# Two lanes of experts in a float32 network: subtractions a piece later, spread products in the lane's own banks, a spaced gather, another order of chunks

## The chip, the cores and the metric

One Trainium2 chip, and of it one core. The metric is the device time of one execution of the whole program in microseconds (us); lower is better. Every matrix product runs on TensorE (PE), elementwise work on VectorE (DVE) and ScalarE (ACT), a little on GpSimd (POOL); SyncE (SP) issues the loads of the weights.

## The reference, cut to what matters

The network is two blocks on 256 tokens of width 1024, in float32. The change touches only its last part, a mixture of eight experts, two of them for each token:

```python
def swiglu(t, w_gate, w_up, w_down):
    return jnp.matmul(jax.nn.silu(jnp.matmul(t, w_gate)) * jnp.matmul(t, w_up), w_down)

def moe_swiglu(h, w_router, w_gate, w_up, w_down):      # t [256, 1024], 8 experts, 3584 hidden
    logits = jnp.matmul(t, w_router)
    top_val, top_idx = lax.top_k(logits, 2)
    gates = jax.nn.softmax(top_val, axis=-1)
    combine = jnp.sum(jax.nn.one_hot(top_idx, 8) * gates[..., None], axis=1)
    for e in range(8):
        out = out + combine[:, e:e + 1] * swiglu(t, w_gate[e], w_up[e], w_down[e])
```

## The kernel before

**Pieces.** The weights of an expert are read in tiles of 128 x 2048 floats, 1 MB, here called pieces. An expert has seven chunks of 512 hidden columns; a chunk is two pieces of the gate weights (`w_eg`), two of the up weights (`w_eu`) and two of the down weights (`w_ed`). All eight experts are 336 pieces. SP loads a piece into one of nine buffers (`raw`). To multiply in float32 precision, a piece is split in two: ACT copies it to `wh`, rounded (L341), and DVE subtracts, `wl = raw - wh` (L342). Both go to "wide" buffers, four of each. PE then multiplies with `wh` and with `wl`. The subtraction is the last reader of `raw`, so it lets SP load the next piece; PE's products are the last readers of the wide buffers, so they let ACT copy the piece four further on.

**Two lanes.** The experts are sorted by the number of their tokens. The first three (`BIG`) are the lane 0, with up to 128 tokens each: PE needs 12 products of 512 columns for a piece (L289 to L291: high by high, low by high, high by low). The other five are lane 1, with up to 64 tokens: high and low part of the tokens stand side by side in the 128 columns of the stationary operand, and a piece takes 8 products (L1164, L1165); their two halves are added by one more product with a constant (`fold`, L1256). `two_lanes` sets the order of the chunks: four chunks of lane 0, then two of lane 1 and one of lane 0 in turn, at the end one of lane 1.

**What follows a chunk.** After a chunk's projections: `silu` on ACT, `times` on DVE (`h`, L1263), four transposes on PE (L1268, into a `tp` bank), and `parts`, which splits the transposed tile into `hT` (ACT, then DVE). The down products of a chunk stand behind the projections of the chunk that follows it, and sum up in two banks (`acc`) for each lane. After an expert's last chunk, for each half of the columns, `scaled` splits the sum into `y` (ACT L344, DVE L345), `spread` multiplies it back to the token rows (PE L1225) and adds it to `x` (DVE L381). The next expert's (or two small experts') tokens are gathered by `collect`: `pick` (a one-hot `G` on DVE), four `turn`s (8 or 16 short products, L1130), four copies to `xg` (ACT), `back` (transposes of `G`, then `gs` and `GT` on DVE).

**Order.** It is written by hand: a list of pieces, and for each piece a list of steps (`at(i, f)`) that come behind it. The driver runs over i; it first issues load, copy and subtraction of piece i + 3, then the products of piece i, then the steps listed for i. `in_order` chains the instructions of PE, ACT and DVE in just that order, so an engine never overtakes an instruction that waits.

**PSUM banks.** Four `acc` (two for each lane), two `pr` (projections), two `tp`. The transposes, the gather, `back` and `spread` share the two `tp` banks.

Of the kernel before, what the change touches and what calls it, by code (L numbers as in the profile page):

```python
# [193 lines left out]
class Net:  # L194
# [53 lines left out]
    def piece(self, ap, w=2048, scales=None, pool=None, fine=False):  # L248
# [5 lines left out]
        with ExitStack() as st:  # L254
# [754 lines left out]
    def moe(self, R):  # L1009
# [12 lines left out]
        with ExitStack() as st:  # L1022
# [16 lines left out]
            v.tensor_scalar(g1, g2, 1.0, None, op0=OP.add)  # L1039
            v.reciprocal(g1, g1)  # L1040
            v.tensor_tensor(g2, g2, g1, op=OP.mult)
            v.tensor_tensor(comb, sel, oh0, op=OP.subtract)
            v.tensor_tensor(comb, comb, b2(g2), op=OP.mult)
            v.tensor_tensor(oh0, oh0, b2(g1), op=OP.mult)
            v.tensor_tensor(comb, comb, oh0, op=OP.add)
# [6 lines left out]
            for ins, n in zip((R.scored[1, 1], R.counted), self.dummies):  # L1052
                self.keep_warm(R.xh[:, 0, :P], R.xh[:, 0, :512], (ins,), n)
            first = self.gather_first(self.slot(0), G, comb)
# [3 lines left out]
            v.tensor_scalar(c1[:, 1:], count[:, 1:], 1.0, None, op0=OP.mult)  # L1058
            v.tensor_scalar(c1[:, :1], count[:, :1], float(2 * T), None, op0=OP.add)
            place = self.places(c1)  # L1060
# [4 lines left out]
            v.tensor_tensor(which, index[:, :, None].to_broadcast([P, NE, NE]), place[:, None, :].to_broadcast([P, NE, NE]),  # L1065
                            op=OP.is_equal)
            v.tensor_tensor(prod[:, 0], which, index[:, None, :].to_broadcast([P, NE, NE]), op=OP.mult)
            v.tensor_reduce(ids, prod[:, 0], axis=AX.X, op=OP.add)
            v.tensor_copy(idi, ids)
            kcp = mo.tile([P, 4, NE], F32, name="kcp")  # L1070
            v.tensor_tensor(prod, kc.rearrange("p a t e -> p (a t) e")[:, :, None, :].to_broadcast([P, 4, NE, NE]),
                            which[:, None].to_broadcast([P, 4, NE, NE]), op=OP.mult)
            v.tensor_reduce(kcp, prod, axis=AX.X, op=OP.add)
            self.less = mo.tile([P, NE], F32, name="less")
            v.tensor_scalar(self.less, place, BIG - 0.5, float(P - HALF), op0=OP.is_gt, op1=OP.mult)
            v.tensor_tensor(c1, count, self.less, op=OP.add)
            most = mo.tile([P, 1], F32, name="most")
            v.tensor_reduce(most, c1, axis=AX.X, op=OP.max)
            mosti = mo.tile([P, 1], I32, name="mosti")
            v.tensor_copy(mosti, most)  # L1080
            self.experts(first, idi, kcp[:, :2], kcp[:, 2:])
# [22 lines left out]
    def back(self, G, comb, k, dt):  # L1104
# [8 lines left out]
        GT = mo.tile([P, T], dt, name="GT", bufs=5)  # L1113
# [28 lines left out]
    def gather_first(self, slot, G, comb):  # L1142
# [4 lines left out]
        return [((slot[:, :KB], slot[:, KB:]),) + self.back(G[:, :, 0], comb, 0, F32R)]  # L1147
# [31 lines left out]
    def experts(self, first, idi, key, comb):  # L1179
# [4 lines left out]
        ids, found = {0: 0}, {0: first[0]}  # L1184
# [11 lines left out]
        def collect(small, k, i):  # L1196
# [4 lines left out]
            def pick():  # L1201
                s["G"], s["x"] = self.pick(key, k, n, small), self.slot(small)
# [7 lines left out]
            def back(e):  # L1210
                x = s["x"].rearrange("p (e k) m -> p k e m", e=2)[:, :, e] if small else (s["x"][:, :KB], s["x"][:, KB:])
                found[k + e] = (x,) + self.back(s["G"][:, :, e], comb, k + e, F32R)

            at(i, pick)
            for j in range(4):
                at(i + 1 + j, lambda j=j: turn(j))
# [343 lines left out]
```

## Time and profile before

| what | value |
|---|---|
| median of 3 runs | 1823.81 us (1821.02 to 1824.0) |
| the profiled execution: its own time | 1823.72 us |
| its span, from first to last instruction | 1821.6 us |
| mean granted TensorE clock | 0.979 of 2.4 GHz |
| busy: PE, DVE, ACT | 1733.0, 1502.6, 1247.2 us |
| part of the experts: first product to last split in the pattern | about 903 to 1784 us of the span |

Times in the rows below count from the start of the span. "Busy" of PE is modelled: its matmuls are pipelined, and a row's duration is longer than the distance to the next one. DMA share is the mean busy share of the 16 DMA engines; a wait in square brackets is the engine's idle time before an instruction and what ended it.

### The profile page before, as it was taken

The page shows a single profiled execution, that of the slowest core. Times are in us where ns is not written, and L with a number is a line of the kernel's source. Part 1 is how long each engine was busy: PE and PEld are TensorE (multiplying, and loading weights), DVE is VectorE, ACT ScalarE, POOL GpSimd, SP SyncE. Part 2 cuts the span into 40 slices and gives each one's busy share as a digit, 9 for nine tenths or more (in the row PEclk, how much of TensorE's full clock was granted, in tenths as well). Part 3 has the DMA queues.
Part 4 walks back from the last instruction along what each step waited for, and adds up shares of the span by engine and source line. Part 5 has one row for each costly group of instructions (what it writes and reads, how often), then busy time and mean ns, then how long its engine had stood idle before and what let it go on. Part 6 is the DMA issues. An engine that isn't in the chain of part 4 may idle for free.

```text
span 1821.6 us, 23787 instructions
## 1 busy us (share of the span) xinstructions
PE 1733.0 (95%) x8735; PEld 1435.8 (79%) x8735; DVE 1502.6 (82%) x1659; ACT 1247.2 (68%) x1412; POOL 159.0 (9%) x120
## 2 busy tenths in 40 slices
PE   8999999999999999999999999899999989999996
PEld 6888778888888889998787777677777767777774
DVE  7577668777766579996689998899999988999997
ACT  5574456555655565655478887698888867888885
POOL 1033010002000024660100000000000000000000
PEclk9999999999999999999899999999999989999998
DMA  8433455554555554337389999899999989999992
GB/s 281 161 116 139 162 191 185 187 191 154 178 185 188 176 190 139 126 127 299 144 313 372 421 421 400 305 412 422 393 392 414 421 308 360 420 421 367 420 421 86
DMA packets 72141, 501.30 MB, mean 275 GB/s; under 512 B 8257, under 2 KB 9281, under 8 KB 13266
## 3 DMA queue, kind: packets, MB, share of 16 engines
q1 hardware_dynamic: 72018, 499.71, 71.7%
q8 instruction: 71, 1.16, 0.2%
q14 instruction: 52, 0.43, 0.1%
HBM read 498.63 MB, written 1.05 MB: 274 GB/s over the span
## 4 chain that ended last, share of the span: by engine, by line
PE 75%; DVE 14%; issue 7%; ACT 3%; POOL 1%; DMA 0%; SPq 0%; DVEq 0%; ACTq 0%
DVE wl L342 8%; PE acc L289 7%; PE acc L291 7%; PE acc L290 7%; PE pr L289 5%; PE pr L291 5%; PE pr L720 5%; PE tp L720 5%; PE pr L290 5%; PE pr L1164 4%; PE pr L1165 4%; PE acc L1164 4%; PE acc L1165 3%; PE tp L721 2%; PE pr L721 2%
## 5 line engine op out<-in xcount | busy, mean ns | idle before, releaser
L342 DVE TENSOR_TENSOR wl<-raw,wh 128x2048 fp32r<-128x2048 f32 (+2 forms) x588 | 1061.8, 1833 | 166.4 <-ACT wh L341 162.8
L341 ACT ACTIVATE wh<-raw 128x2048 fp32r<-128x2048 f32 (+2 forms) x596 | 892.6, 1521 | 231.3 <-PE acc L291 74.7
L1164 PE MATMUL pr<-wh,xg 128*128 128x512 f32 x560 | 228.4, 408 | 0.0
L1165 PE MATMUL pr<-wl,xg 128*128 128x512 f32 x560 | 224.8, 401 | 0.0
L289 PE MATMUL pr<-wh,xg 128*128 128x512 f32 x336 | 137.7, 410 | 0.0
L1164 PE MATMUL acc<-wh,hT 128*128 128x512 f32 x280 | 115.4, 412 | 23.0 <-DVE hT L342 23.0
L291 PE MATMUL pr<-wh,xg 128*128 128x512 f32 x336 | 134.6, 401 | 0.0
L290 PE MATMUL pr<-wl,xg 128*128 128x512 f32 x336 | 134.6, 401 | 0.0
L1164 PEld LDWEIGHTS pr<-wh,xg 128*128 128x128 f32 x560 | 107.4, 192 | 25.5
L720 PE MATMUL pr<-xT,wh 128*128 128x512 f32 x352 | 125.4, 399 | 1.9 <-DVE xT L342 1.9
L1165 PEld LDWEIGHTS pr<-wl,xg 128*128 128x128 f32 x560 | 107.4, 192 | 24.4
L720 PE MATMUL tp<-xT,wh 128*128 128x512 f32 x352 | 125.3, 399 | 0.0
L1165 PE MATMUL acc<-wl,hT 128*128 128x512 f32 x280 | 113.6, 406 | 0.0
L289 PE MATMUL acc<-wh,xT 128*128 128x512 f32 (+3 forms) x256 | 98.8, 387 | 1.9 <-ACT xT L341 1.1
L721 PE MATMUL tp<-xT,wl 128*128 128x256 f32 x352 | 98.9, 281 | 0.0
L721 PE MATMUL pr<-xT,wl 128*128 128x256 f32 x352 | 98.8, 281 | 0.0
L291 PE MATMUL acc<-wh,xT 128*128 128x512 f32 (+3 forms) x256 | 98.6, 387 | 0.2
L290 PE MATMUL acc<-wl,xT 128*128 128x512 f32 (+3 forms) x256 | 98.3, 385 | 0.0
L1164 PEld LDWEIGHTS acc<-wh,hT 128*128 128x128 f32 x280 | 54.9, 196 | 41.6 <-DVE hT L342 29.1
L1423 POOL TENSOR_TENSOR raw<-x,raw 128x512 f32<-128x512 f32 x2 | 2.5, 1286 | 916.5 <-DVE x L381 916.5
L720 PEld LDWEIGHTS pr<-xT,wh 128*128 128x128 f32 x352 | 66.1, 188 | 18.6 <-DVE xT L342 2.4
L720 PEld LDWEIGHTS tp<-xT,wh 128*128 128x128 f32 x352 | 66.1, 188 | 16.5
(373 smaller groups left out, 3344.4 us busy)
## 6 DMA issues: line engine op xcount, KB each, us to landing
raw<-in_w_eg SPq DMA_DIRECT2D x112, 1024.0 KB, 7.9
raw<-in_w_eu SPq DMA_DIRECT2D x112, 1024.0 KB, 8.0
raw<-in_w_ed SPq DMA_DIRECT2D x110, 1024.0 KB, 8.0
raw<-in_w_ffn_in SPq DMA_DIRECT2D x22, 1024.0 KB, 4.8
raw<-in_w_dense_in SPq DMA_DIRECT2D x22, 1024.0 KB, 4.8
raw<-in_w_xbc SPq DMA_DIRECT2D x16, 1024.0 KB, 5.0
raw<-in_w_ffn_out SPq DMA_DIRECT2D x11, 1024.0 KB, 4.9
raw<-in_w_dense_out SPq DMA_DIRECT2D x11, 1024.0 KB, 4.8
```

Of the source, the lines that this page charges most:

```text
L289: mm(ps, st[0], mv[0], start=start, stop=False)
L290: mm(ps, st[0], mv[1], start=False, stop=False)
L291: self.last_mm = mm(ps, st[1], mv[0], start=False, stop=stop)
L341: a = nc.scalar.activation(h, src, AF.Copy)
L342: b = v.tensor_tensor(l, src, h.bitcast(F32), op=OP.subtract)
L720: nc.tensor.matmul(ps, wh, xT[2][:, k], start=k == 0, stop=False)
L721: nc.tensor.matmul(ps[:, 0], wl, xT[0][:, k], start=False, stop=k == KB - 1)
L1164: self.nc.tensor.matmul(ps, st, mv[0], start=start, stop=False)
L1165: self.nc.tensor.matmul(ps, st, mv[1], start=False, stop=stop)
L1423: nc.gpsimd.tensor_tensor(xn[:, t, lo], self.x[:, t, lo], g[:, lo], op=OP.mult)
```

## The change

Six edits, all in the experts' part.

1. **apart.** In `piece`, ACT's copy is issued with piece i + 3 as before, but the subtraction is put off: it is issued one piece later, behind the next piece's copy. The first four pieces, which are split in halves (`gates`), stay as they were.
2. **two_lanes.** Two chunks of lane 0 first, then for each small expert 1,1,0,1,1,0,1,1,0,1,0 (the last 0 dropped). Before, the first big expert and the first small one ended with the 13th and the 14th chunk; now with the 16th and the 12th. The second big one ended with the 34th and a small one with the 35th; now the 35th and the 34th.
3. **spread.** In the pattern it writes to the lane's own two `acc` banks instead of `tp`; `y` has four buffers instead of two; `scaled` and `spread` come 1, 2, 3 and 6 pieces after the first down piece instead of 1, 5, 4 and 8.
4. **collect.** The four `turn`s stand two pieces apart instead of one, `back` follows at 9 (and 10) instead of 5 (and 6).
5. **parts** of a small chunk come behind piece 7 instead of 8. `GT` has 4 buffers instead of 5.
6. **sort.** The sorting of the experts and the gate values (`comb`), some 25 small DVE instructions ahead of the list before, stand together at i = -1 now; the first expert's `back` moves into the list, and the first small `collect` to piece 1 instead of 8.

```diff
+                if apart:
+                    self.nc.scalar.activation(ab[0], raw, AF.Copy)
+                    return Weight(hw, [ab[0][:, :hw], ab[0][:, hw:]], [ab[1][:, :hw], ab[1][:, hw:]]), \
+                        lambda: v.tensor_tensor(ab[1], raw, ab[0].bitcast(F32), op=OP.subtract)
...
-        rest = (NE - BIG) * EC
-        n = rest // 2
-        lane = [0] * (BIG * EC - n) + [1, 1, 0] * n + [1] * (rest - 2 * n)
+        runs = [2] * (EC // 2) + [1] * (EC % 2)
+        lane = [i for _ in range(NE - BIG) for r in runs for i in [1] * r + [0]][:-1]
+        lane = [0] * (BIG * EC - lane.count(0)) + lane
...
-                at(i + 1 + j, lambda j=j: turn(j))
-                at(i + 2 + j, lambda j=j: copy(j))
+                at(i + 1 + 2 * j, lambda j=j: turn(j))
+                at(i + 2 + 2 * j, lambda j=j: copy(j))
             for e in range(n):
-                at(i + 5 + e, lambda e=e: back(e))
+                at(i + 9 + e, lambda e=e: back(e))
...
-                ps = self.tp()
+                ps = banks[t] if banks else self.tp()
...
-            y = [mo.tile([P, 512], F32R, name="y%d" % b) for b in range(2)]
+            y = [mo.tile([P, 512], F32R, name="y%d" % (2 * n + b)) for b in range(2)]
...
-                when = (2, 3, 4, 4, 5, 5, 7, 8)
+                when = (2, 3, 4, 4, 5, 5, 7, 7)
...
-                    at(i + 1 + 4 * n, lambda n=n, y=y: y.update(y=scaled(small, k, n)[0]))
-                    at(i + 4 + 4 * n, lambda n=n, y=y: spread(k, n, y["y"]))
+                    at(i + 1 + n, lambda n=n, y=y: y.update(y=scaled(small, k, n)[0]))
+                    at(i + 3 + 3 * n, lambda n=n, y=y: spread(k, n, y["y"], accs[small]))
...
-        collect(1, BIG, 8)
-        ahead, ready = self.wholes - 1, {}
+        collect(1, BIG, 1)
+        at(1, lambda: found.update({0: found[0] + self.back(G[:, :, 0], self.comb, 0, F32R)}))
+        ahead, ready, rest = self.wholes - 1, {}, {}
         for i in range(-ahead, len(pieces)):
-            if i + ahead < len(pieces):
-                ready[i + ahead] = pieces[i + ahead][0]()
+            a = i + ahead
+            if a < len(pieces):
+                if self.gates:
+                    ready[a] = self.piece(pieces[a][0]())
+                else:
+                    ready[a], rest[a] = self.piece(pieces[a][0](), apart=True)
+            if a - 1 in rest:
+                rest.pop(a - 1)()
+            if i == -1:
+                sort()
```

On DVE, in the pattern, the order before is (`h` of 64 rows is a small chunk's, `hT` of 128x4x64 its split, `wl` a subtraction):

```order
L342 TENSOR_TENSOR wl<-raw,wh 128x2048 x5
L1263 TENSOR_TENSOR h<-h,pr 64x512
L342 TENSOR_TENSOR wl<-raw,wh 128x2048 x3
L342 TENSOR_TENSOR hT_9384<-tp,hT_9384 128x4x64
L342 TENSOR_TENSOR wl<-raw,wh 128x2048 x3
L1263 TENSOR_TENSOR h<-h,pr 64x512
```

and the same stretch of the pattern in the changed kernel (L267 is the subtraction put off, L346 the split of `hT`):

```order
L267 TENSOR_TENSOR wl<-raw,wh 128x2048 x5
L1274 TENSOR_TENSOR h<-h,pr 64x512
L267 TENSOR_TENSOR wl<-raw,wh 128x2048 x2
L346 TENSOR_TENSOR hT_9448<-tp,hT_9448 128x4x64
L267 TENSOR_TENSOR wl<-raw,wh 128x2048 x4
L1274 TENSOR_TENSOR h<-h,pr 64x512
```

Two subtractions stand between `h` and a small `hT` instead of three; and as every subtraction has moved behind one piece's steps, `h` now follows the subtraction of two pieces ahead of PE, not of three.

On DVE again, where the first big expert ends, the order before is (two lanes' `y` and `x` interleaved):

```order
L345 SCALAR_TENSOR_TENSOR y_10460<-acc,gs,y_10459 128x512
L342 TENSOR_TENSOR wl<-raw,wh 128x2048 x2
L345 SCALAR_TENSOR_TENSOR y_10496<-acc,gs,y_10495 128x512
L1263 TENSOR_TENSOR h<-h,pr 64x512
L342 TENSOR_TENSOR wl<-raw,wh 128x2048
L381 TENSOR_TENSOR x<-x,tp 128x512 x2
L342 TENSOR_TENSOR wl<-raw,wh 128x2048 x2
L381 TENSOR_TENSOR x<-x,tp 128x512 x2
```

and where an expert first ends in the changed kernel:

```order
L349 SCALAR_TENSOR_TENSOR y_10186<-acc,gs,y_10185 128x512
L267 TENSOR_TENSOR wl<-raw,wh 128x2048
L349 SCALAR_TENSOR_TENSOR y_10210<-acc,gs,y_10209 128x512
L346 TENSOR_TENSOR hT_10214<-tp,hT_10213 128x512
L267 TENSOR_TENSOR wl<-raw,wh 128x2048
L385 TENSOR_TENSOR x<-x,acc 128x512 x2
L267 TENSOR_TENSOR wl<-raw,wh 128x2048 x3
L385 TENSOR_TENSOR x<-x,acc 128x512 x2
```

The additions read `acc` now, and one expert's four steps stand alone.

## Rows read from the trace of the kernel before

**Rows 1.** The page's head: span and instructions.
```profile
span 1821.6 us, 23787 instructions
```

**Rows 2.** Stretches: from:to, length, busy us of each engine (instructions), PEclk, DMA share, GB/s.
```profile
903.00:1784.00 881.00, 832.20 (x3675) 659.15 (x3675) 815.58 (x523) 723.11 (x549) 0.00 (x0) 0.98 0.97 388
903.00:975.00 72.00, 72.00 (x337) 59.01 (x337) 56.74 (x58) 49.31 (x39) 0.00 (x0) 0.97 0.87 312
1115.00:1180.00 65.00, 55.80 (x232) 43.50 (x231) 55.86 (x40) 46.52 (x38) 0.00 (x0) 0.95 0.89 326
1295.00:1335.00 40.00, 36.85 (x171) 29.49 (x171) 37.62 (x29) 33.78 (x29) 0.00 (x0) 1.00 0.97 367
1455.00:1530.00 75.00, 65.80 (x258) 50.97 (x257) 62.79 (x42) 52.41 (x42) 0.00 (x0) 0.89 0.87 320
1640.00:1680.00 40.00, 37.04 (x158) 29.36 (x157) 38.51 (x25) 33.32 (x26) 0.00 (x0) 0.96 0.97 359
```

**Rows 3.** The same view: the five stretches between those, summed.
```profile
sum 589.00, PE 564.72 PEld 446.82 DVE 564.06 ACT 507.78 POOL 0.00; mean PE 112.94 PEld 89.36 DVE 112.81 ACT 101.56 POOL 0.00
```

**Rows 4.** DVE's groups, 903 to 1784: busy, mean ns | idle before, releaser.
```profile
L342 DVE TENSOR_TENSOR wl<-raw,wh 128x2048 fp32r<-128x2048 f32 x328 | 736.9, 2284 | 53.5 <-ACT wh L341 53.1
...
L381 DVE TENSOR_TENSOR x<-x,tp 128x512 f32<-128x512 f32 x24 | 15.9, 682 | 7.0 <-PE tp L1225 7.0
...
L345 DVE SCALAR_TENSOR_TENSOR y<-acc,gs,y 128x512 fp32r<-128x512 f32 x12 | 9.0, 746 | 4.3 <-ACT y L344 4.3
```

**Rows 5.** Timeline of DVE in the pattern: start, us, what, idle before.
```profile
1003.84 4.48 DVE L342 TENSOR_TENSOR wl<-raw,wh 128x2048 fp32r<-128x2048 f32 x2
...
1012.03 2.29 DVE L342 TENSOR_TENSOR wl<-raw,wh 128x2048 fp32r<-128x2048 f32 x1 [0.81 <-ACT wh L341]
1014.24 0.68 DVE L1263 TENSOR_TENSOR h<-h,pr 128x512 f32<-128x512 f32 x1
...
1022.04 11.09 DVE L342 TENSOR_TENSOR wl<-raw,wh 128x2048 fp32r<-128x2048 f32 x5
...
1047.79 4.48 DVE L342 TENSOR_TENSOR wl<-raw,wh 128x2048 fp32r<-128x2048 f32 x2
```

**Rows 6.** Timeline of PE: opening, first small piece, products in the pattern.
```profile
902.71 0.73 PE L289 MATMUL pr<-wh,xg 128*128 128x512 f32 x1
...
973.49 0.48 PE L1164 MATMUL pr<-wh,xg 128*128 128x512 f32 x1
...
1001.31 0.39 PE L291 MATMUL pr<-wh,xg 128*128 128x512 f32 x1
...
1001.54 0.40 PE L289 MATMUL pr<-wh,xg 128*128 128x512 f32 x1
...
1012.40 0.40 PE L291 MATMUL pr<-wh,xg 128*128 128x512 f32 x1
```

**Rows 7.** DMA, 1000 to 1100; landing of `raw`, 1000 to 1030, 1060 to 1090.
```profile
DMA packets 5780, 42.09 MB, mean 421 GB/s; under 512 B 646, under 2 KB 646, under 8 KB 646
...
DMA to landing us min/median/max: 7.7/8.4/9.1
...
DMA to landing us min/median/max: 8.9/9.9/10.7
```

**Rows 8.** Waits, 1115 to 1180: us in total, times, longest.
```profile
PE tp L1225 <- DVE x L381: 6.7, 3, 3.1
...
ACT y L344 <- PE tp L1225: 5.7, 2, 3.7
...
PE tp L1268 <- DVE x L381: 2.5, 1, 2.5
```

**Rows 9.** Timeline of ACT and of DVE: a small chunk's `hT`.
```profile
1008.46 0.36 ACT L341 ACTIVATE hT<-tp 128x256 fp32r<-128x256 f32 x1
...
1010.80 0.42 DVE L342 TENSOR_TENSOR hT<-tp,hT 128x256 fp32r<-128x256 f32 x1
```

**Rows 10.** Tile `idi` (the sorted experts): SP's loads, ns min/median/max, first and last.
```profile
L1193 SPq TENSOR_LOAD <-idi x7: 262/272/473, 924.7 to 929.2; - x7
```

More of the change, by code (lines that the diff above doesn't have):

```diff
@@ L246, in fetch, with piece @@
         return raw
-    def piece(self, ap, w=2048, scales=None, pool=None, fine=False):
+    def piece(self, ap, w=2048, scales=None, pool=None, fine=False, apart=False):
         raw = ap.tile if isinstance(ap, Loaded) else self.fetch(ap, w)
@@ L1073, in moe, with sort @@
-            v.tensor_reduce(kcp, prod, axis=AX.X, op=OP.add)
             self.less = mo.tile([P, NE], F32, name="less")
-            v.tensor_scalar(self.less, place, BIG - 0.5, float(P - HALF), op0=OP.is_gt, op1=OP.mult)
-            v.tensor_tensor(c1, count, self.less, op=OP.add)
             most = mo.tile([P, 1], F32, name="most")
-            v.tensor_reduce(most, c1, axis=AX.X, op=OP.max)
             mosti = mo.tile([P, 1], I32, name="mosti")
-            v.tensor_copy(mosti, most)
-            self.experts(first, idi, kcp[:, :2], kcp[:, 2:])
+            def sort():
+                v.tensor_scalar(c1[:, 1:], count[:, 1:], 1.0, None, op0=OP.mult)
+                v.tensor_scalar(c1[:, :1], count[:, :1], float(2 * T), None, op0=OP.add)
+                place = self.places(c1)
+                v.tensor_tensor(which, index[:, :, None].to_broadcast([P, NE, NE]), place[:, None, :].to_broadcast([P, NE, NE]),
+                                op=OP.is_equal)
+                v.tensor_tensor(prod[:, 0], which, index[:, None, :].to_broadcast([P, NE, NE]), op=OP.mult)
+                v.tensor_reduce(ids, prod[:, 0], axis=AX.X, op=OP.add)
+                v.tensor_copy(idi, ids)
+                v.tensor_scalar(g1, g2, 1.0, None, op0=OP.add)
+                v.reciprocal(g1, g1)
+                v.tensor_tensor(g2, g2, g1, op=OP.mult)
+                v.tensor_tensor(comb, sel, oh0, op=OP.subtract)
+                v.tensor_tensor(comb, comb, b2(g2), op=OP.mult)
+                v.tensor_tensor(oh0, oh0, b2(g1), op=OP.mult)
+                v.tensor_tensor(comb, comb, oh0, op=OP.add)
+                v.tensor_tensor(prod, kc.rearrange("p a t e -> p (a t) e")[:, :, None, :].to_broadcast([P, 4, NE, NE]),
+                                which[:, None].to_broadcast([P, 4, NE, NE]), op=OP.mult)
+                v.tensor_reduce(kcp, prod, axis=AX.X, op=OP.add)
+                v.tensor_scalar(self.less, place, BIG - 0.5, float(P - HALF), op0=OP.is_gt, op1=OP.mult)
+                v.tensor_tensor(c1, count, self.less, op=OP.add)
+                v.tensor_reduce(most, c1, axis=AX.X, op=OP.max)
+                v.tensor_copy(mosti, most)
@@ L1082, in moe @@
+            self.experts(first, sort, idi, kcp[:, :2], kcp[:, 2:])
             need = nc.values_load(mosti[0:1, 0:1], min_val=0, max_val=T + P)
@@ L1177, in two_lanes, with experts @@
             yield small, BIG * small + k, c
-    def experts(self, first, idi, key, comb):
+    def experts(self, first, sort, idi, key, comb):
         nc, mo, mm = self.nc, self.mo, self.nc.tensor.matmul
@@ L1183, in experts @@
         accs = [[self.acc() for _ in range(2)] for _ in range(2)]
-        ids, found = {0: 0}, {0: first[0]}
+        slot, G = first
+        ids, found = {0: 0}, {0: ((slot[:, :KB], slot[:, KB:]),)}
         pieces, later, chunks = [], {}, list(self.two_lanes())
@@ L1201, in pick @@
             def pick():
-                s["G"], s["x"] = self.pick(key, k, n, small), self.slot(small)
+                s["G"], x = self.pick(key, k, n, small), self.slot(small)
+                s["x"] = x
+                for e in range(n):
+                    found[k + e] = (x.rearrange("p (e k) m -> p k e m", e=2)[:, :, e] if small else (x[:, :KB], x[:, KB:]),)
             def turn(j):
```

34 lines of the change are left out of this document (8 added, 26 removed).

## The prediction

> **What bounds the kernel now.** I read first the head of the page [rows 1], then the stretches of the experts' part [rows 2, 3], and inside them DVE's groups and timeline, PE's timeline, the transfers and the waits. The profiled execution took 1823.72 us for a span of 1821.6, so 2.1 us lie around the span; it stands 0.1 us below the median, 1823.81, and sums against it need no correction. Less than 0.2%, 3.6 us, cannot be told from no change here.
>
> From 903 to 1784 three things are nearly full at once. DVE is busy 815.6 of 881 us [rows 2]. The load runs at 421 GB/s wherever nothing disturbs it [rows 7], that is 1.0486 MB / 421 GB/s = 2.49 us a piece. PE's products of 512 columns start 0.233 us apart (1001.31, 1001.54) [rows 6], so a big piece is 12 x 0.233 = 2.80 us and a small one 8 x 0.233 = 1.87 us.
>
> In the pattern the period of 18 pieces is 1047.79 - 1003.84 = 43.95 us, 2.44 a piece [rows 5]. PE needs 12 x 1.87 + 6 x 2.80 = 39.2 us of it and four folds and three sets of transposes (an estimate from the same spacing: 2), DVE 18 subtractions of 11.09 / 5 = 2.22 us and its small ones, about 43. So DVE sets the pace there, a little faster than the load supplies (18 x 2.49 = 44.8). The reader sees this in the landing times, 8.4 us around 1015 and 9.9 us around 1075 [rows 7]: the loads queue up, and the stock of landed pieces melts by some 2%. No one waits for data yet.
>
> The loss stands elsewhere. DVE's idle time is 881 - 815.6 = 65.4 us: 15.3 in the opening (72 us), 24.9 in the five undisturbed stretches (589 us, 4.2%), 9.1 + 12.2 = 21.3 in the two stretches in which a big and a small expert end together (140 us), 2.4 + 1.5 = 3.9 in the two in which a small one ends alone (80 us) [rows 2, 3]. Almost all of it, 53.1 us, is a subtraction waiting for ACT's copy [rows 4]. The load falls with it: 312, 326, 320 GB/s, and 367 and 359 where one ends alone.
>
> **Opening.** 22 big pieces stand ahead of the first small product: 902.71 to 973.49 is 70.8 us [rows 6], of which 22 x 2.80 = 61.6 are products. PE is busy all 72 us [rows 2], so here PE sets the pace. In the new order 12 of the first 22 pieces are big and 10 small: PE saves 10 x 4 x 0.233 = 9.3 us. The ten big pieces that move come later in the pattern, where eleven chunks need 42 x 1.87 + 24 x 2.80 = 145.7 us and about 7.5 of folds and transposes, 153 of 66 x 2.44 = 161: still hidden behind DVE, with 5% to spare (6% before); without that cover they would cost the 9.3 back. As DVE has 22 x 2.22 = 48.8 us of subtractions and some 8 of small work (the sort, `G`, `GT`, `h`, `hT`) in what are then 61 us, most of the saving counts. I take 8, bounds 4 and 9.3. The sort now stands in a block ahead of the fourth piece: about 25 instructions of 0.1 to 0.2 us, 3 us, in a time in which the opening has 15.3 us of idle DVE. SP needs the sorted ids for the 11th piece instead of the 23rd; its seven loads of them are 0.27 us each and start between 924.7 and 929.2 [rows 10], so about 5 us of SP are moved ahead of loads that PE multiplies 25 us later: nothing, at worst 3.
>
> **Where experts end.** In the first double stretch PE waits 6.7 + 2.5 us for DVE's additions before it gets a `tp` bank, and ACT stands 5.7 us before `y` because the buffer of the other lane's `y` is not yet read [rows 8]; behind ACT's `y` the copies queue, and behind them DVE's subtractions. The lane's own banks remove the first wait, four `y` buffers the second. What cannot be removed is DVE's work itself, 4 x 0.68 + 2 x 0.75 = 4.2 us for an expert [rows 4]. Of the 21.3 us of idle time, 4.2% of 140, 5.9, is what an undisturbed stretch has too; 15.4 is the stall. I take 13, bounds 6 and 15.4; in the second place the two experts still end in neighbouring chunks, but their steps no longer interleave. The single ends have 3.9 - 3.4 = 0.5 to give: nothing.
>
> **Ends apart.** With ends spread over more places, the stock can carry a part of each: a landing of 9.9 us against 8.4 is 1.5 us of queue that DVE may fall behind without a loss of load [rows 7]. Two more single places, 1.5 each: 3, bounds 0 and 6.
>
> **Subtraction later, `parts` earlier.** The subtractions among themselves keep their order; `h`, `hT`, `y` and the additions come one subtraction, 2.2 us, earlier on DVE, a small `hT` two. PE gets them earlier, and wide buffers are free earlier. In the undisturbed stretches the load is at its ceiling, so I take 0 there. Upper bound: the 24.9 us of idle time there, of which the load leaves at most some 14 (388 GB/s over 881 us are 342 MB [rows 2], at 421 that is 812 us, so 69 us of load are lost in all; of them go the 24 summed up below, and some 30 that DVE's own work where experts end and PE's in the opening must cost). Lower bound: a big `h` is ready at 1012.80 and starts at 1014.24, 1.44 us of slack [rows 5, 6] against 2.2: 0.76 us of stall for each of 21 big chunks, 16 us. A small `hT` is ready at 1008.82 and starts at 1010.80, 1.98 us [rows 9], against 4.4. But ACT's half of that split also comes a piece earlier, and a PE that no longer waits for `hT` delivers `h` earlier.
>
> **Spaced gather, tail.** The same instructions; four `turn`s no longer stand behind four pieces in a row. 0, bounds -1 and 1. The tail from 1784 on keeps its chain: 0, bounds 0 and 2.
>
> **Sum.** 8 + 13 + 3 + 0 = 24 us: 1823.7 - 24 = 1799.7, 1800.
>
> **A page's ceiling.** At 421 GB/s the load needs 812 us for what comes after 903, so it leaves the forecast's 857 us alone [rows 2, 7]. The Trainium skill says otherwise: "DMA: Bandwidth & Descriptors", section "Where 436 GB/s comes from", holds that for loads from HBM a core's share of HBM, about 358 GB/s, binds, and not the fabric's 435. By 358 those 342 MB would take 955 us, the load would be the bound today, and the change would bring nothing (1824); the 421 GB/s of this trace contradict it, and the trace decides, so that rival has no chance. By 435 the load would need 786 us.
>
> **Rivals.**
> - *More than forecast.* With `hT` earlier PE never holds the copies up, and DVE's idle time in the undisturbed stretches shrinks as well. For: 53.1 us of DVE's idle are waits for copies, which wait for PE. Against: load at 421 GB/s. Another 14: 1786. Chance 0.18.
> - *The stock runs out.* Without the stops the stock never refills, ACT waits for data, and the period goes from 43.95 to 44.8. Over 14 of some 16 periods that is 12 us back: 1812. For: landing times that rise. Against: the total leaves room. Chance 0.14.
> - *The stall moves.* The ends still stall, on DVE's `x` or on `y`, and the opening's saving is spent on the sort: 1822. Against: each wait in rows 8 names a resource that is now separate. Chance 0.06.
> - *Slower: DVE waits for PE.* `h` and `hT` ahead of a subtraction make DVE idle, queued behind them are the subtractions that free `raw` and feed PE. With 16 us for big `h` and 2.4 us for every second of 35 small `hT`, partly covered, 20: 36 against a gain of 24, 1836. It decides from 24 / 112 = 0.21 us a step on (two steps in 56 chunks). For: the slacks above. Against: today's chain already makes DVE idle 0.81 us right there [rows 5]. Chance 0.10.
>
> **Numbers.** The forecast, 1800, has 0.52, with an own range of 1790 to 1810. The range of 1779 to 1820 takes in the better case with some room, the case of the stock, and leaves out the slower case, most of the moved stall and the far end of the better one. Faster (below 1820.2) 0.84, same 0.06, slower 0.10.
>
> **What would show it.** Right: first small product about 33 us after the first product (10 x 2.80 and the gather) instead of 71; no wait of PE's `spread` on DVE; no ACT wait before `y`; load above 370 GB/s where the big experts end; DVE idle about 40 us in the experts' part. Wrong: DVE waits for `pr` or `tp` before `h`, `hT` or `x`; ACT waits for `raw`; PE at a clock below 1 in new places. The rows of the order cannot tell which comes last, only the trace can; the weakest step is the 0 for the later subtraction.

## The result, and the profile after

The changed kernel takes 1772.84 us (median of 4 runs, 1768.34 to 1773.79) beside 1823.9 us for the kernel before in the same runs: a ratio of 0.9717, 95% interval 0.9697 to 0.9737. It is 51 us faster; the forecast had 24. The direction was right, and the time lies below the range.

The head of the page after:

```profile
span 1770.8 us, 23849 instructions
```

The span is 50.8 us shorter than in [rows 1]. The experts' part now runs from 903 to 1735, 832 us instead of 881 [rows 2]; the tail behind it has 35.8 us instead of 37.6. So 49 of the 50.8 us are in the experts' part. The stretches of it, with the columns of [rows 2]:

```profile
903.00:1735.00 832.00, 823.51 (x3678) 644.19 (x3677) 811.08 (x516) 721.98 (x548) 0.00 (x0) 1.00 1.00 411
903.00:960.00 57.00, 57.00 (x272) 46.64 (x271) 47.79 (x47) 43.26 (x37) 0.00 (x0) 0.97 0.88 329
960.00:1080.00 120.00, 119.11 (x518) 92.27 (x517) 119.82 (x67) 108.39 (x80) 0.00 (x0) 1.00 1.01 421
1080.00:1260.00 180.00, 177.39 (x802) 138.75 (x801) 175.33 (x115) 154.12 (x120) 0.00 (x0) 1.00 1.01 420
1260.00:1420.00 160.00, 158.33 (x699) 122.86 (x698) 158.12 (x96) 140.24 (x105) 0.00 (x0) 1.00 1.00 410
1420.00:1480.00 60.00, 59.58 (x281) 47.81 (x281) 58.86 (x46) 51.23 (x43) 0.00 (x0) 1.00 1.01 413
1480.00:1580.00 100.00, 98.68 (x433) 76.22 (x431) 99.93 (x58) 91.06 (x68) 0.00 (x0) 1.00 1.01 421
```

The third busy number is DVE's. Its idle time in the whole part is 832 - 811.1 = 20.9 us, against 65.4 before: 44.5 of the 49 us. The other 4.5 is less busy time of DVE in this stretch: part of the sort stands ahead of 903 now, one whole subtraction fewer falls in it, and subtractions that follow each other without a wait overlap a little (2284 ns each, but 2.22 us apart). Where experts end (their additions stand between 1103 and 1284, between 1437 and 1466, and between 1606 and 1617) the load keeps 410 to 420 GB/s, where [rows 2] had 320 to 367. In slices of 20 us its lowest rate between 960 and 1720 is 373 GB/s (1280 to 1300), where the kernel before fell to 266 (1480 to 1500). And in a stretch without ends, 1480 to 1580, DVE is busy 99.93 of 100 us; the undisturbed stretches of before had 564.06 of 589 [rows 3]. That last difference is what the forecast did not have.

DVE's groups, 903 to 1735, in the columns of [rows 4]:

```profile
L267 DVE TENSOR_TENSOR wl<-raw,wh 128x2048 fp32r<-128x2048 f32 x327 | 730.5, 2284 | 0.0
L1274 DVE TENSOR_TENSOR h<-h,pr 64x512 f32<-64x512 f32 (+1 forms) x55 | 37.5, 682 | 7.7 <-PE pr L295 6.8 <-PE pr L1267 0.3
L346 DVE TENSOR_TENSOR hT<-tp,hT 128x256 fp32r<-128x256 f32 (+1 forms) x55 | 28.6, 520 | 8.9 <-ACT hT L345 8.9
L385 DVE TENSOR_TENSOR x<-x,acc 128x512 f32<-128x512 f32 x24 | 15.4, 683 | 0.0
L349 DVE SCALAR_TENSOR_TENSOR y<-acc,gs,y 128x512 fp32r<-128x512 f32 x12 | 8.9, 746 | 1.1 <-ACT y L348 1.1
```

A subtraction takes what it took, 2284 ns, but 327 of them wait for ACT's copy 0.0 us in all, where 328 waited 53.5 [rows 4]. DVE now waits for `h` and `hT` instead, 7.7 + 8.9 us.

DVE's timeline in the pattern, as [rows 5]:

```profile
1495.67 0.69 DVE L1274 TENSOR_TENSOR h<-h,pr 64x512 f32<-64x512 f32 x1
1496.26 4.50 DVE L267 TENSOR_TENSOR wl<-raw,wh 128x2048 fp32r<-128x2048 f32 x2
1500.67 0.43 DVE L346 TENSOR_TENSOR hT<-tp,hT 128x256 fp32r<-128x256 f32 x1
1501.00 8.90 DVE L267 TENSOR_TENSOR wl<-raw,wh 128x2048 fp32r<-128x2048 f32 x4
1509.81 0.69 DVE L1274 TENSOR_TENSOR h<-h,pr 64x512 f32<-64x512 f32 x1
...
1538.49 0.68 DVE L1274 TENSOR_TENSOR h<-h,pr 64x512 f32<-64x512 f32 x1
```

From 1495.67 to 1538.49 is one period of 18 pieces: 42.82 us, against 43.95 [rows 5]. The small `hT` stands behind two subtractions, and there is no idle time at any row.

PE's timeline, first product and first small product, as [rows 6]:

```profile
902.12 0.73 PE L293 MATMUL pr<-wh,xg 128*128 128x512 f32 x1
...
937.07 0.48 PE L1171 MATMUL pr<-wh,xg 128*128 128x512 f32 x1
```

That is 35 us after the first product (71 before, 33 foretold). The loads of the sorted ids by SP, as [rows 10]:

```profile
L1202 SPq TENSOR_LOAD <-idi x7: 266/273/470, 902.8 to 908.0; - x7
```

They moved 21 to 22 us ahead, at the same cost. All waits of PE that are over 1 us in total, 903 to 1735, as [rows 8]:

```profile
PE pr L1172 <- DVE wl L267: 4.1, 13, 0.7
PE acc L294 <- DVE wl L267: 2.5, 3, 1.0
```

No product of `spread` and no transpose waits for DVE's additions any more. ACT's largest waits:

```profile
ACT wh L265 <- PE pr L295: 37.7, 50, 4.2
ACT hT L345 <- PE tp L1279: 36.6, 34, 2.2
```

`y` does not occur among ACT's waits. The second row had 2.9 us before: `parts` comes a piece earlier, so ACT is at the small `hT` before PE's transposes are. ACT is busy 722 of 832 us and can afford it.

### The profile page after: what moved, and what is told of

It is laid out like the page before. It is cut to its first block, busy times and chain, and to the rows that moved or that the text cites. A ratio compares the mean times of both kernels' runs of the same rounds, so it can differ in the third digit from the quotient of the medians.

```text
span 1770.8 us, 23849 instructions
## 1 busy us (share of the span) xinstructions
PE 1723.5 (97%) x8735; PEld 1421.2 (80%) x8735; DVE 1498.3 (85%) x1659; ACT 1245.9 (70%) x1412; POOL 159.1 (9%) x120
## 4 chain that ended last, share of the span: by engine, by line
PE 57%; DVE 30%; issue 9%; ACT 3%; POOL 1%; DMA 1%; SPq 0%; DVEq 0%; ACTq 0%
DVE wl L267 21%; PE acc L293 7%; PE acc L294 7%; PE acc L295 7%; PE pr L724 5%; PE tp L724 5%; PE pr L293 3%; PE pr L295 2%; PE pr L294 2%; PE pr L725 2%; PE tp L725 2%; PE pr L1172 2%; PE pr L1171 2%; DVE wl L346 2%; PE acc L470 1%
## 5 line engine op out<-in xcount | busy, mean ns | idle before, releaser
L267 DVE TENSOR_TENSOR wl<-raw,wh 128x2048 fp32r<-128x2048 f32 x330 | 737.2, 2284 | 0.0
L265 ACT ACTIVATE wh<-raw 128x2048 fp32r<-128x2048 f32 x330 | 620.9, 1912 | 71.0 <-PE pr L295 37.7
L346 DVE TENSOR_TENSOR wl<-raw,wh 128x1024 fp32r<-128x1024 f32 (+2 forms) x258 | 320.9, 1257 | 114.6 <-ACT wh L345 111.8
L345 ACT ACTIVATE wh<-raw 128x1024 fp32r<-128x1024 f32 (+3 forms) x266 | 271.3, 1036 | 93.3 <-PE acc L295 62.0
L1171 PE MATMUL pr<-wh,xg 128*128 128x512 f32 x560 | 225.1, 402 | 0.0
L293 PE MATMUL pr<-wh,xg 128*128 128x512 f32 x336 | 136.3, 406 | 0.0
L295 PE MATMUL pr<-wh,xg 128*128 128x512 f32 x336 | 133.4, 397 | 0.0
L1172 PEld LDWEIGHTS pr<-wl,xg 128*128 128x128 f32 x560 | 105.2, 188 | 34.2 <-DVE wl L267 11.3
L1171 PE MATMUL acc<-wh,hT 128*128 128x512 f32 x280 | 111.4, 398 | 0.0
```

The lines of the kernel that those rows point to most:

```text
L265: self.nc.scalar.activation(ab[0], raw, AF.Copy)
L267: lambda: v.tensor_tensor(ab[1], raw, ab[0].bitcast(F32), op=OP.subtract)
L293: mm(ps, st[0], mv[0], start=start, stop=False)
L295: self.last_mm = mm(ps, st[1], mv[0], start=False, stop=stop)
L345: a = nc.scalar.activation(h, src, AF.Copy)
L346: b = v.tensor_tensor(l, src, h.bitcast(F32), op=OP.subtract)
```

## The experiments

**The theory.** One wait had been passed over. It is the largest of PE's in the kernel before, 903 to 1790 (total, times, longest):

```profile
PE acc L1164 <- DVE hT L342: 23.0, 14, 2.0
```

and one of the 14 in PE's timeline (the wait in square brackets):

```profile
1040.72 0.50 PE L1164 MATMUL acc<-wh,hT 128*128 128x512 f32 x1 [1.95 <-DVE hT L342]
```

with ACT and DVE around it, from their timelines of the same kernel:

```profile
1035.85 0.36 ACT L341 ACTIVATE hT<-tp 128x256 fp32r<-128x256 f32 x1
...
1042.65 3.79 ACT L341 ACTIVATE wh<-raw 128x2048 fp32r<-128x2048 f32 x2 [0.85 <-PE acc L1164]
```

```profile
1033.65 6.68 DVE L342 TENSOR_TENSOR wl<-raw,wh 128x2048 fp32r<-128x2048 f32 x3
1040.25 0.41 DVE L342 TENSOR_TENSOR hT<-tp,hT 128x256 fp32r<-128x256 f32 x1
```

ACT's half of the split is done at 1036.21. DVE's half stands behind three subtractions, until 1040.25, and PE, which has come to the down products, stops for 1.95 us. The delay goes on: PE frees wide buffers later, ACT's copy waits 0.85 us for PE, and later subtractions wait for copies. So DVE pays, some pieces on, for its own order. The theory: this loop costs the undisturbed stretches their 25 us of idle DVE, and more where it meets the ends. Either the later subtraction or the earlier `parts` opens it, and DVE's work then sets the time. This theory was put down for the runs from e5 on. The first four runs had another, theory S of the expectations below, which had only the later subtraction remove DVE's waits for copies. The rivals: that the stock of landed pieces pays for the gain; that the load, at 421 GB/s, sets the time; that banks and order are worth far more than forecast.

The ratios below are to the kernel before in the same runs, with 95% intervals.

| run | edit | us | ratio |
|---|---|---|---|
| (after) | the change | 1772.84 | 0.9717 (0.9697 to 0.9737) |
| e1_no_apart | after, subtraction with its copy again | 1777.12 | 0.9741 (0.9713 to 0.9769) |
| e11_apart_parts8 | after, `parts` behind piece 8 again | 1771.90 | 0.9700 (0.9683 to 0.9718) |
| e6_no_apart_parts8 | after, both undone | 1802.48 | 0.9884 (0.9861 to 0.9906) |
| e2_before_apart | before, later subtraction alone | 1786.07 | 0.9797 (0.9770 to 0.9825) |
| e5_before_parts7 | before, `parts` behind piece 7 alone | 1800.62 | 0.9870 (0.9847 to 0.9893) |
| e14_before_banks | before, banks and four `y` alone | 1806.58 | 0.9914 (0.9885 to 0.9942) |
| e13_before_order | before, order of chunks alone | 1818.35 | 0.9972 (0.9957 to 0.9987) |
| e15_before_gather | before, spaced gather alone | 1817.03 | 0.9955 (0.9938 to 0.9973) |
| e3_spread_tp | after, `spread` in `tp` | 1777.22 | 0.9742 (0.9714 to 0.9770) |
| e4_old_lanes_tp | the same, and the old order | 1780.31 | 0.9769 (0.9740 to 0.9798) |
| e9_four_first | after, four big chunks first | 1771.32 | 0.9696 (0.9680 to 0.9712) |
| e10_dense_gather | after, dense gather | 1778.05 | 0.9737 (0.9721 to 0.9753) |
| e7_seven_raw | after, seven `raw` instead of nine | 1775.69 | 0.9739 (0.9716 to 0.9763) |
| e12_less_load | after, 56 of 336 loads left out | 1772.52 | 0.9698 (0.9682 to 0.9715) |
| e8_half_sub_ed | after, half of each `w_ed` subtraction left out | 1762.06 | 0.9661 (0.9633 to 0.9689) |
| e16_pool_share | after, every ninth subtraction on GpSimd | 1842.39 | 1.0109 (1.0088 to 1.0131) |

### The subtraction and `parts`

**e1_no_apart**

```diff
-                    ready[a], rest[a] = self.piece(pieces[a][0](), apart=True)
+                    ready[a] = self.piece(pieces[a][0]())
```

> The changed kernel with one edit undone: each subtraction is issued with its own copy again. Theory S (the later subtraction takes away DVE's waits for ACT's copy also in the undisturbed stretches, 24.9 us before; DVE then runs ahead of the load, the queue of loads fills between the ends, and pays for DVE's work there): DVE idle in the experts' part back to 45 to 50 us, time 1795 to 1805. Theory L (the order of the chunks, the own banks and the ends apart carry the gain, the later subtraction is worth nothing): 1773 to 1780, DVE idle near 21 us.

This is some 4 us slower than the changed kernel (0.9741 beside 0.9717, with intervals that overlap), where theory S had 22 to 32. PE's wait for `hT` does not come back, since `parts` stands early; DVE waits for copies again, though:

```profile
DVE wl L346 <- ACT wh L345: 18.3, 25, 1.9
```

**e2_before_apart**: the new `piece` and the driver's lines in the kernel before.

```diff
-                ready[i + ahead] = pieces[i + ahead][0]()
...
+                    ready[a], rest[a] = self.piece(pieces[a][0](), apart=True)
+            if a - 1 in rest:
+                rest.pop(a - 1)()
```

> The kernel before with the later subtraction alone. Theory S: 1793 to 1803, the waits of subtractions for copies (53 us) fall below 20 us, the load stays at 421 GB/s longer; the two double ends and the opening still cost. Theory L: 1818 to 1825. If later h and hT steps now wait for PE instead (the slower rival of the prediction): above 1826.

One edit of six gives 0.9797, 37 us, more than the forecast for all and more than theory S had. Three of PE's waits in it:

```profile
PE tp L1229 <- DVE x L385: 9.5, 6, 2.5
PE tp L1272 <- DVE x L385: 5.2, 4, 1.9
...
PE acc L1168 <- DVE hT L346: 0.8, 2, 0.4
```

`hT` has gone from 23.0 to 0.8 us; the waits at the experts' ends are still there.

**e5_before_parts7**

```diff
-                when = (2, 3, 4, 4, 5, 5, 7, 8)
+                when = (2, 3, 4, 4, 5, 5, 7, 7)
```

> The kernel before with one number changed: parts of a small chunk behind piece 7 instead of 8, so that its hT stands one subtraction earlier on DVE. Theory H (the wait that set the pace of the undisturbed stretches is PE's for a small hT, 23 us in 14 waits before; it delays PE, so ACT's copies, so DVE's subtractions; either the later subtraction or the earlier parts removes it): PE's waits for hT gone, DVE idle in the undisturbed stretches (975 to 1115) from 5.6 to below 2 us, time 1785 to 1800. Theory S' (only moving the subtraction behind the next copy frees DVE; the first run's smaller loss came from the order of chunks): 1815 to 1824.

One number gives 0.9870, 24 us. The gain can be seen to arise: a big chunk's `h` on DVE starts 0.62 us earlier than in the kernel before at 969.09 (968.47), 1.86 at 1014.24 (1012.38) and 3.10 at 1058.17 (1055.07), a step of 1.24 us a period. No PE wait for the down products' `hT` is left in it, and DVE still waits 41.8 us for copies, since a subtraction stands right behind its copy:

```profile
DVE wl L342 <- ACT wh L341: 41.8, 52, 5.8
```

**e6_no_apart_parts8**, in the changed kernel:

```diff
-                when = (2, 3, 4, 4, 5, 5, 7, 7)
+                when = (2, 3, 4, 4, 5, 5, 7, 8)
...
-                    ready[a], rest[a] = self.piece(pieces[a][0](), apart=True)
+                    ready[a] = self.piece(pieces[a][0]())
```

> The changed kernel with both undone: subtraction with its copy, and parts behind piece 8. Order of chunks, own banks, y buffers, spaced gather and early sort stay. Theory H: PE waits for small hT again, the undisturbed stretches fall back to DVE idle near 4%: 1790 to 1802, and that is what the other edits are worth alone (some 24 us, the prediction's sum). Theory L (order and banks carry the gain): 1775 to 1782.

With both undone, banks, order, gather and sort give 21 us, and PE's wait is back (903 to 1763), as is DVE's for copies, 42.7 us:

```profile
PE acc L1171 <- DVE hT L346: 24.7, 15, 2.0
```

**e11_apart_parts8**: of these two, the line of `when` alone.

> The changed kernel, with the split of a small chunk behind piece 8 again. Theory (the loss was PE's wait for the small split, and either the later subtraction or the earlier split takes it away): the later subtraction covers it alone, PE's wait for the split stays below 6 us (22.7 where both are undone), 1773 to 1778. Rival (the earlier split is worth some 20 us whatever the subtractions do, as it was alone on the kernel before): 1790 or more, with PE's wait back near 20 us.

Nothing is lost. PE waits 1.4 us for the small `hT`:

```profile
PE acc L1171 <- DVE hT L346: 1.4, 4, 0.6
```

So the two edits stand in for each other: from 1802.5 either one brings 1777.1 (`parts`) or 1771.9 (subtraction), both 1772.8. The order of chunks is the same with both undone and with both, so their timelines can be laid beside each other. With both undone DVE's first `h` starts 3.3 us earlier (913.77, 917.10) and its last one 30.0 us later (1774.49, 1744.46), and from one big `h` to the next the distance grows by 1.1 us in the pattern: 1.18 (1020.24, 1019.06), then 2.31 (1064.18, 1061.87).

### What sets the time now

**e7_seven_raw**

```diff
-    def __init__(..., rings=(3, 1, 4, 1), ...):
+    def __init__(..., rings=(3, 1, 2, 1), ...):
```

> The changed kernel with seven raw buffers instead of nine (two fewer in the third ring). Theory S on the ends (the queue of loads, 10 to 14 us deep before an end, pays for DVE's 4 to 8 us of work there): with two buffers less, 5 us of load, the queue is at most some 8 us deep, and each of five ends costs 2 to 4 us: 1780 to 1795, load below 400 GB/s around each end. Rival (DVE alone sets the time, it is 97% busy, and the depth of the queue does not matter): within 3 us of 1773.

ACT now does wait for data, 20.4 us in the three weights, of which the largest is

```profile
ACT wh L265 <- DMA raw<-in_w_ed: 9.7, 20, 0.6
```

and the time rises by 3 us, within what the intervals tell. The last two of nine buffers are not what paid for the gain; that the stock of landed pieces plays no part is not shown, since seven buffers hold one too.

**e12_less_load**: the second down piece of a chunk is split from the first one's buffer, so that half of the down weights (the second piece of each chunk) is left out of the computation.

```diff
+            def down_raw(n):
+                if n == 0:
+                    held[0] = Loaded(self.fetch(self.at("w_ed", number(k), 2 * c)))
+                return held[0]
...
-                pieces.append((lambda n=n: self.at("w_ed", number(k), 2 * c + n),
+                pieces.append((lambda n=n: down_raw(n),
```

> The changed kernel without every second load of the down weights: the second down piece of a chunk is split and multiplied from the first one's buffer, so 56 of 336 loads are left out, with the copies, subtractions and products all there (the second half of the down weights is left out of the computation). If DVE's 811 of 832 us set the time: 1769 to 1773, with the load's rate down to some 345 GB/s and DVE's idle time about 20 us. If the load at 411 to 421 GB/s sets the time (812 of 832 us at its ceiling): up to DVE's own bound, 1755 or less, with DVE's idle time below 8.

The stretch of the experts' part, as [rows 2]:

```profile
903.00:1735.00 832.00, 823.40 (x3679) 644.26 (x3679) 811.81 (x520) 722.47 (x549) 0.00 (x0) 1.00 0.92 344
```

344 GB/s, and the same DVE and, by the medians, the same time to 0.3 us. The load does not set the time of the changed kernel.

**e8_half_sub_ed**: of the down weights, DVE subtracts the first half of a piece only, and PE takes the high part in place of the low one for the second; that part of the split is left out.

```diff
+                    if apart == "half":
+                        return Weight(hw, [ab[0][:, :hw], ab[0][:, hw:]], [ab[1][:, :hw], ab[0][:, hw:]]), \
+                            lambda: v.tensor_tensor(ab[1][:, :hw], raw[:, :hw], ab[0][:, :hw].bitcast(F32), op=OP.subtract)
```

> The changed kernel; for the down weights DVE subtracts only the first half of the columns, and PE takes the high part in place of the low one for the second half (this leaves out part of the split). DVE has 110 x 1.1 = 121 us less to do, load and PE the same. If the load is next (812 us at 421 GB/s for what comes after 903): 1755 to 1765, load at 421 throughout. If DVE alone binds: 1700 or less. If PE binds (820 us): 1760 to 1770.

```profile
960.00:1080.00 120.00, 119.25 (x523) 93.72 (x522) 104.09 (x68) 109.43 (x80) 0.00 (x0) 1.00 1.01 422
...
903.00:1724.00 821.00, 815.83 (x3676) 646.33 (x3675) 703.19 (x516) 721.07 (x547) 0.00 (x0) 1.00 1.00 415
```

In these stretches of it, DVE has 108 us less to do (703 against 811), and the time falls by 11. So DVE did set the pace, and close behind it stand the others: 415 to 422 GB/s, PE busy 816 of 821.

**e16_pool_share**

```diff
+                    if apart == "pool":
+                        v = self.nc.gpsimd
...
+                    ready[a], put = self.piece(pieces[a][0](), apart="pool" if a % 9 == 4 else True)
+                    if a % 9 == 4:
+                        put()
```

> The changed kernel, with the subtraction of every ninth piece on GpSimd instead of VectorE, issued with its copy (37 of 336; the chip's own time for a half tile there is 2.3 us, so some 4.6 us a piece). If VectorE's 811 of 832 us set the time: 37 x 2.28 = 84 us less for it, and as where half of each down subtraction was left out, 1761 to 1764, with the load at 421 GB/s throughout. Rival (VectorE slows down beside GpSimd, or PE waits for GpSimd's late tiles): 1773 or more, with the mean subtraction of VectorE above 2.28 us or PE waits for GpSimd.

It was meant to use e8's lesson without leaving work out, and it lost 70 us. The subtractions on GpSimd are issued with their copies. GpSimd's and DVE's timelines at one such place:

```profile
1058.48 5.84 POOL L269 TENSOR_TENSOR wl<-raw,wh 128x2048 fp32r<-128x2048 f32 x1 [17.09 <-ACT wh L265]
```

```profile
1055.41 4.47 DVE L269 TENSOR_TENSOR wl<-raw,wh 128x2048 fp32r<-128x2048 f32 x2
1060.24 6.24 DVE L269 TENSOR_TENSOR wl<-raw,wh 128x2048 fp32r<-128x2048 f32 x1 [0.35 <-ACT wh L265]
```

GpSimd ends at 1064.32; DVE's subtraction, begun at 1060.24, ends 2.16 us after that, at 1066.48. Nearly the whole of its usual 2.28 us lies behind GpSimd's end. DVE's mean subtraction is 2597 ns (290 of them) instead of 2284, which gives the saving back, and PE waits for GpSimd's late tiles, 26.4 us at the small pieces and 14.7 at the big ones (903 to 1780):

```profile
PE pr L1174 <- POOL wl L269: 26.4, 16, 2.7
PE pr L296 <- POOL wl L269: 14.7, 8, 2.7
```

### The other edits, one by one

**e14_before_banks**: `spread` in the lane's banks, four `y`, the end's steps at 1, 2, 3 and 5.

```diff
-                    at(i + 1 + 4 * n, lambda n=n, y=y: y.update(y=scaled(small, k, n)[0]))
-                    at(i + 4 + 4 * n, lambda n=n, y=y: spread(k, n, y["y"]))
+                    at(i + 1 + n, lambda n=n, y=y: y.update(y=scaled(small, k, n)[0]))
+                    at(i + 3 + 2 * n, lambda n=n, y=y: spread(k, n, y["y"], accs[small]))
```

> The kernel before, with the spread products in the lane's own two banks, four buffers of y, and the steps of an expert's end 1, 2, 3 and 5 pieces after its first down piece (5 and not 6, since in the old order the lane's next chunk begins there). The forecast's term 13: 1811. Rival (the waits at the ends are covered by the wait for the small split elsewhere, or worth only what the banks are worth in the changed kernel, 4 us): 1818 to 1822.

0.9914, 16 us (10.6 to 21.0), which holds the forecast's 13. **e3_spread_tp** took the banks back in the changed kernel:

```diff
-                    at(i + 3 + 3 * n, lambda n=n, y=y: spread(k, n, y["y"], accs[small]))
+                    at(i + 3 + 3 * n, lambda n=n, y=y: spread(k, n, y["y"]))
```

> The changed kernel with one edit undone: in the pattern spread writes to the two tp banks again (four y buffers and the new places stay). Theory S: with the ends apart only one expert's spread meets the tp banks at a time, and the stock covers a stall of some us: 1773 to 1780. Theory L with the banks as its main part: 1785 to 1790, PE waiting some 3 us for DVE's additions at each end.

There they are worth 4 us, at the edge of what the intervals tell apart.

**e13_before_order**: the new `two_lanes`, and the first small gather at piece 1.

```diff
-        lane = [0] * (BIG * EC - n) + [1, 1, 0] * n + [1] * (rest - 2 * n)
...
+        lane = [i for _ in range(NE - BIG) for r in runs for i in [1] * r + [0]][:-1]
...
-        collect(1, BIG, 8)
+        collect(1, BIG, 1)
```

> The kernel before, with the new order of chunks alone (and the first small gather at piece 1, since the first small chunk now comes at piece 10). The forecast's terms 8 + 3: 1813 to 1815. Rival (the place of a chunk is worth nothing as long as DVE or PE's wait for the small split sets the pace, as the opening by itself was worth nothing in the changed kernel): 1821 to 1826.

5 us (2.4 to 7.8), where the opening's 8 and the ends' 3 were forecast. **e4_old_lanes_tp** undid the order on top of e3 (the first gather stays at piece 1):

```diff
...
+        lane = [0] * (BIG * EC - n) + [1, 1, 0] * n + [1] * (rest - 2 * n)
...
```

> The changed kernel with the old order of chunks (four big first, then two small and one big), and spread in the tp banks, since the own banks do not allow that order. The later subtraction, the y buffers, the spaced gather and the early sort stay. Prediction's terms: the opening 8 us and the double ends some of 13 come back: 1785 to 1795. Theory S alone: opening 8 us, and the double ends only partly (the stock covers 5 us each): 1783 to 1788. Theory L: 1800 and more.

3 us more than e3, not told apart from it, and below all three of its expectations. **e9_four_first** undid the opening alone:

```diff
+        for at in (19, 8):
...
+            del lane[at]
```

> The changed kernel, with four chunks of lane 0 ahead of the first small one again (two of the later places of lane 0 left out); everything else as in the changed kernel. Tells what the shorter opening is worth by itself. The forecast's term (PE sets the pace of the opening, ten big pieces more cost 9.3 us less of PE when they come later): 8 us back, 1781, and DVE's idle time up by about 8 from 20.9. Rival (with the subtractions put off and no wait for the small split, DVE catches up what it lost in the opening, or had least to lose there): 1 to 3 us back, 1774 to 1776.

No difference (1771.3). DVE does fall behind in the opening, busy 123.4 us from 903 to 1040 instead of 127.7, 4.3 us; but between 1080 and 1260 it is busy 178.8 of 180 instead of 175.3. What gave those 3.5 back was not tested. Of the versions that leave no work out, none was told apart from the changed kernel as faster.

**e15_before_gather** and **e10_dense_gather** put the spaced gather in and took it out:

```diff
-                at(i + 1 + j, lambda j=j: turn(j))
+                at(i + 1 + 2 * j, lambda j=j: turn(j))
...
-                at(i + 5 + e, lambda e=e: back(e))
+                at(i + 9 + e, lambda e=e: back(e))
```

> The kernel before, with the gather's four sets of products two pieces apart and the transposes of the one-hot tile at the ninth piece. The forecast's term 0: 1822 to 1825. Rival (it was worth 5 us in the changed kernel, where a dense gather made DVE wait 8.5 us for those transposes): 1817 to 1820.

> The changed kernel, with the gather's four sets of products one piece apart again and the transposes of the one-hot tile at the fifth piece behind. The forecast's 0, bounds -1 and 1: 1772 to 1774. Rival (PE now has little slack between the pieces, so four sets of short products behind four pieces in a row hold ACT and DVE up at each of five small and two big experts, some 0.5 us each): 1776 to 1777.

Alone it gives 8 us (4.9 to 11.3), and without it the changed kernel loses 6 against the two neighbours of the same runs that equal it (1771.9, 1772.5). The row for the loss in e10:

```profile
DVE gs L1121 <- PE tp L1118: 8.5, 6, 2.5
```

DVE waits for the transposes of `G`, which PE comes to late behind four sets of short products. In the kernel before that wait is 0.6 us, so what the spaced gather saves there is open.

## Why the prediction was wrong

**The failed step.** "In the undisturbed stretches the load is at its ceiling, so I take 0 there." The runs put 30 us in its place: 1802.5 without later subtraction and earlier `parts`, 1772.8 with them. Not all of the 30 lies in those stretches, but there a period fell from 43.95 to 42.82 us. Two things were wrong in the step. First, 421 GB/s over a stretch was read as the limit of that stretch, though the working itself had DVE a little faster than the load there. The load still has 421, but DVE now uses up 18 pieces in 42.82 us, which is 441 GB/s, and the difference comes out of pieces that landed before. It shows in the time from issue to landing of `raw` in the changed kernel, 960 to 1000 and 1040 to 1080:

```profile
DMA to landing us min/median/max: 6.6/8.7/10.0
...
DMA to landing us min/median/max: 11.6/12.6/13.6
```

From 1160 to 1200, where an expert ends, the median is back at 7.2 us. And the stage had room for this, since 342 MB at 421 need 812 of the 881 us. With a sixth of the loads left out the changed kernel takes the same time. The upper bound of 14 rested on the same thought, that some 30 us of load "must" be lost at the ends and in the opening; at the ends the load now runs at 410 to 420 GB/s.

Second, in the sum the 24.9 us of idle DVE there [rows 3] were traced to ACT's copy [rows 4] and no further. One question more, what the copy waits for, leads to PE (the first rival came that far), and one after that to `hT` on DVE. [rows 9] showed half of it, `hT` on ACT at 1008.46 and on DVE at 1010.80. The working took the 1.98 us between them as slack of DVE and did not ask who was waiting at the other end. At that place a big chunk's products keep PE busy meanwhile; where two small chunks follow each other, DVE's half began 4.04 us after ACT's was done (1036.21, 1040.25), and PE stood 1.95 us.

**The rest of the sum.** Without that step 24 us were forecast and 21 came (17 to 25). The terms one by one on the kernel before: banks and `y` 16 for 13, order 5 for 8 + 3, gather 8 for 0. Together 29 beside 21 for all at once, so they seem to overlap, though the intervals nearly allow that they do not. The close agreement of the sum is partly luck: opening and ends apart were put too high, the gather too low. The early sort was not run by itself. The tail gave 1.8, within its 0 to 2.

**What was to be seen.** Right: the first small product (35 us for 33), no wait of `spread` on DVE's additions (one of 0.4 us on `y` is left), none of ACT before `y`, over 370 GB/s in the stretches with the big experts' ends (420 and 413). Wrong: DVE idle 20.9 us, not 40. The text named the 0 for the later subtraction as its weakest step, and it was.

**The rivals.** *More than forecast* was the case, with the mechanism in the right place ("with `hT` earlier PE never holds the copies up") and less than half its size. *The stock runs out* did not happen, though the landing times rise as it said: the kernel can even do with two buffers fewer. *Slower* saw waits that are real: DVE now stands 6.8 us for `pr` before `h` and 8.9 us for ACT's half before `hT`, 15.7 together, 10 us of it behind 960. The first is one of the prediction's signs of being wrong. They are less than the waits for copies that they replaced. Why the exchange is so uneven is argued and not tested: DVE ahead of PE loses the difference once, while a late `hT` stopped PE, and through the buffers ACT and DVE again. *The stall moves* is out.

**The clock.** One rival stands on neither list, the prediction's or that of the experiments. TensorE's granted clock was 0.98 in the experts' part before and 0.89 in the second double end [rows 2]; after, it is 1.00. At the falls looked at here PE had just waited, but not every wait was followed by one: that at 1040.72 was not. Another of the 14 waits for `hT` in the kernel before was:

```profile
1084.65 0.79 PE L1164 MATMUL acc<-wh,hT 128*128 128x512 f32 x1 [1.96 <-DVE hT L342]
1085.23 0.63 PE L1165 MATMUL acc<-wl,hT 128*128 128x512 f32 x1
1085.66 0.63 PE L1164 MATMUL acc<-wh,hT 128*128 128x512 f32 x1
```

The products start 0.43 us apart instead of 0.233: this is the lower of the two levels, 1.2 GHz, and it lasted until 1088. Added up over slices of 10 us from 933 on, what is missing to the full clock comes to 17 us before, 15 in e5, 15 in e6, 5 in e1 and nothing in e11 and in the changed kernel. So e5's 24 us came with the clock nearly as low as before, and the clock is not what they are made of. From e6 to the changed kernel both the waits and the slow products went, and no run separates the two: how much of the 30 us the clock gave back is open.

**The ceiling.** The Trainium skill ("DMA: Bandwidth & Descriptors", "Where 436 GB/s comes from") gives about 358 GB/s as binding for loads from HBM. The experts' part, on the one core that ran, now holds 411 GB/s over 832 us, so the measurement decides here too.

## What to carry to other kernels

Follow each wait two or three steps back, until it comes to an instruction that waits for nothing: on three nearly full engines that run in order, a small instruction behind three large ones on the engine that sets the pace can stop the others and come back as that engine's own idle time. A transfer rate at its ceiling within a stretch does not bound the stage: compare the bytes at that rate with the time of the whole, here 812 of 881 us. And price an edit on the kernel in which it will stand: later subtraction and earlier `parts` were worth 37 and 24 us alone on the kernel before, and 30 together on top of the other edits.

## What the hardware showed beyond that

In e16 a subtraction of DVE, both operands in SBUF, hardly moved while GpSimd ran another: 6.24 us instead of 2.28, ending 2.16 us after GpSimd's. The Trainium skill says this in "GPSIMD Engine Reference", section "1. Specifications": GpSimd shares its SBUF interfaces with VectorE, and VectorE instructions with two SBUF inputs contend with it there. The trace agrees, and adds that it was nearly a full stop at this place. It went the other way as well: a subtraction of GpSimd that began at 1353.13, while four of DVE's followed each other until 1358.43, took 9.72 us and ended 4.42 us after them; DVE's four took 8.88 us, as they do alone. In all, one whole tile took GpSimd 4.6 to 9.7 us (mean 6.1 of 37). The 4.6 that had been worked out from a half tile's 2.3 is the shortest of them.
